# A two-layer decoder trunk on one core: GpSimd gives up its elementwise work, a norm of the second token tile goes to ScalarE, and the block behind a norm runs its matmul passes in another order

## The chip, the cores and the metric

The kernel runs on one core of one Trainium2 chip. The metric is device time in microseconds of one execution, the median of several runs.

The engines are called by these names: PE is TensorE (matmuls and transposes; PEld is its weight load), DVE is VectorE, ACT is ScalarE, POOL is GpSimd, SP is SyncE, whose queue (SPq) issues the transfers. Each engine works through its own queue in order.

## The reference, cut to what matters

256 tokens of 2048 channels pass two layers. Every sub-layer ends in a norm of the residual sum.

```
layer 0:  h = LN(a*h + [pool_mixer | stick_breaking_attention] @ even_w_out)
          h = LN(a*h + (silu(h @ Wg) * (h @ Wu)) @ Wd)                 # 5632 wide
layer 1:  h = LN(a*h + spatial_gating(gelu(h @ odd_w_in)) @ odd_w_out)
          logits = h @ w_router ; the two largest of 8, softmax over them -> gates
          h = LN(a*h + sum_e gates[:, e] * swiglu_e(h))                # 1408 wide
LN(x) = (x - mean) * rsqrt(var + 1e-5) * g + b,    a = 4 ** 0.25,  all in float32
```

## The kernel before, in words

The 256 tokens are two tiles of 128 (t = 0 and 1; `h0_1534` and `h1_1535` in the order's rows). Each product in float32 precision is made of three passes. A chunk of weights, up to 4 k-slices of 128 x 512, comes by a transfer on SP into `raw`. ScalarE rounds it to the head `wh` (L109), VectorE takes the remainder `wl = raw - wh` (L117). The activations are split the same way into `xh` (L161) and `xl` (L162). For each k-slice TensorE runs head times head (L126), head times weight remainder (L127) and activation remainder times weight head (L128). There are 5 `raw` buffers, 4 each of `wh` and `wl`, 4 PSUM tiles for sums (`acc`) and 4 for the rest (`ps`).

A *block* is one tile's 16 k-slices against one chunk column of 512: 48 matmuls, four groups (kg0 to kg3) of four k-slices. Blocks follow each other through all stages, so TensorE only waits where a block's operands come late. That is at the three places where a norm lies between two matmuls:

- **A**, the start of the FFN (about 300 to 340 us): tile 0 is normed while tile 1's last out-projection block still runs. The first FFN block (tile 0) starts while tile 1's norm is done. `ln_to_lhs` normalises a quarter `h` (L239), transposes it on TensorE (L168), scales it on ScalarE and splits it into `xh` and `xl`. Each of the four quarters q0 to q3 holds the four k-slices of one group.
- **B**, the start of the SGU (about 1036 to 1080 us): the same.
- **C**, the start of the experts (about 1328 to 1375 us): the router's logits, top-2, a one-hot matrix `Dt` (L795) of the sorted tokens, and then a gather: matmuls of the tokens' head and remainder (`xth`, `xtl`, made by `token_parts`, L619 and L620) with `Dt` (L813), whose result ScalarE casts to the experts' `xe` (L815). `keep_busy` (L886) issues matmuls on constants there.

A scheduler sets the order within each engine's queue from the program's order and its own due times. `self.plan` is the hand on it: each entry is popped by one `load` and says behind which instruction that chunk's `wl` may stand (a fence without a semaphore, `after`) and on which engine it is made. After a norm of tile 0 the second chunk's `wl` goes to GpSimd as two 128x1024 pieces (A, B and C). In the experts' down projection, the third chunk of each column has three k-slices: VectorE takes two of them, GpSimd the last (`tail=HALF`, 32 chunks). GpSimd also makes five of the eight `xtl`, scales one quarter of tile 1 in C, and does 5 of the 12 multiplications and additions of the final norm behind the last matmul (L744 and L745).

Of the kernel before, what the change touches and what calls it, by code (L numbers as in the profile page):

```python
# [22 lines left out]
CB = 512  # L23
# [8 lines left out]
PIECE = 4  # L32
HALF = 2
FINAL_POOL = ((1, 3), (1, 3))
FINAL_POOL2 = ((1,), ())
RSQRT_MAGIC = float(0x5F3759DF)
# [38 lines left out]
class Trunk:  # L75
# [22 lines left out]

    def load(self, src, w=CB, tail=None):

        nc = self.nc
        fence, planned = self.plan.pop(0) if self.plan else (None, nc.vector)
        src = src.rearrange("p (k n) -> p k n", n=w)
        kc = src.shape[1]
        raw = self.praw.tile([P, kc, w], F32, tag="raw", name="raw")
        wh = self.pw.tile([P, kc, w], F32R, tag="wh", name="wh")
        wl = self.pw.tile([P, kc, w], F32R, tag="wl", name="wl")
        nc.sync.dma_start(raw, src)
        nc.scalar.copy(wh, raw)  # L109
        if tail is not None:  # L110
            cuts = [(0, tail, nc.vector), (tail, kc, nc.gpsimd)]
        elif planned is nc.gpsimd:
            cuts = [(k, min(k + HALF, kc), planned) for k in range(0, kc, HALF)]
        else:
            cuts = [(0, kc, planned)]
        for a, b, eng in cuts:
            self.after(eng.tensor_tensor(wl[:, a:b, :], raw[:, a:b, :], wh[:, a:b, :].bitcast(F32), ALU.subtract),  # L117
                       fence)
        return wh, wl, kc
# [4 lines left out]
    def mm3(self, acc, xh, xl, wh, wl, first, last):  # L124
        mm = self.nc.tensor.matmul
        mm(acc, xh, wh, start=first, stop=False)  # L126
        mm(acc, xh, wl, start=False, stop=False)  # L127
        mm(acc, xl, wh, start=False, stop=last)  # L128

    def blocks(self, groups, lhs, tiles, w=CB, between=None, at=8):  # L130
# [94 lines left out]
    def ln_to_lhs(self, t, stats, which, xT):  # L225

        nc = self.nc
        mean, rstd = self.rstd(stats)
        self.plan += [(self.last, nc.vector)] * (6 if t else 1)
        if t == 0:  # L230
            self.plan += [(None, nc.gpsimd)]
        gc, bc = self.lncols[:, 2 * which, :], self.lncols[:, 2 * which + 1, :]
        for half in range(2):
            xh = self.unit("xh")
            xl = self.unit("xl")
            for q in range(2):
                n = half * 2 + q
                hs = self.h[t][:, n * CB:(n + 1) * CB]
                nc.vector.tensor_scalar(hs, hs, mean, rstd, ALU.subtract, ALU.mult)  # L239
                ps = self.transpose4(hs).rearrange("p (c t) -> p c t", c=4)  # L240
                f = self.pln.tile([P, 4, P], F32, tag="lnT", name="lnT")
                for j in range(4):
                    c = n * 4 + j
                    nc.scalar.activation(f[:, j, :], ps[:, j, :], AF.Identity, bias=bc[:, c:c + 1],
                                         scale=gc[:, c:c + 1])
                self.split_evac(f, xh[:, q * 4:q * 4 + 4, :], xl[:, q * 4:q * 4 + 4, :])
            xT[t, half] = (xh, xl)
# [218 lines left out]
    def ffn(self, xT, G, B, norm):  # L466
# [3 lines left out]
        with self.pool("ffn", side="right") as pf:  # L470
            def gate_up(j):
                accs = {}
                hT = {}
                for u in range(2):
                    groups = self.loads(i["even_ffn_gu"][j, u])
                    for t in range(NT):
                        accs[u, t] = self.block(groups, lhs, t)
                        if j == 1 or (j == 0 and u == 1):
                            self.flush(self.lo_ins)
                        if u == 1:  # L480
                            hT[t] = self.swiglu(pf, accs[0, t], accs[1, t], CB, 4, "f")
                return hT
# [39 lines left out]
    def sgu(self, xT, G0, B0):  # L522
# [3 lines left out]
        with self.pool("sgu", side="right") as pg:  # L526
# [8 lines left out]
            for n in range(8):  # L535
# [8 lines left out]
                for t in range(NT):  # L544
                    acc = self.block(groups, lhs, t)
                    if n < 4:
# [69 lines left out]

    def token_parts(self, src, dst, q, eng):
        cs = slice(q * CB, (q + 1) * CB)
        self.nc.scalar.copy(dst[0][:, cs], src)  # L619
        eng.tensor_tensor(dst[1][:, cs], src, dst[0][:, cs].bitcast(F32), ALU.subtract)  # L620

    def moe(self, pm, stats, G, B):
# [13 lines left out]
        for t in range(NT):  # L636
            mean, rstd = self.rstd(stats[t])
            if t == 0:
                self.plan += [(self.last, nc.vector), (None, nc.gpsimd)]
            nmr = self.nmr(mean, rstd)  # L640
            hs = [self.h[t][:, n * CB:(n + 1) * CB] for n in range(NCB)]
            if t:
                for n in (0, 2, 1, 3):
                    nc.scalar.activation(hs[n], hs[n], AF.Identity, bias=nmr, scale=rstd)
                nc.gpsimd.tensor_tensor(hs[2], hs[2], G[2], ALU.mult)
                nc.gpsimd.tensor_tensor(hs[2], hs[2], B[2], ALU.add)
            lrow = pm.tile([P, NEXP], F32, tag="lrow", name="lrow", bufs=1)
# [5 lines left out]
            if t == 0:  # L653
                for n in range(NCB):
                    self.ln_apply(hs[n], mean, rstd, G[n], B[n])
                    self.token_parts(hs[n], xtok[t, n // 2], n % 2, nc.gpsimd)
        fence = self.last
        self.plan += [(fence, nc.vector)] * 2
        self.keep_busy(8, self.c[:, :CB // 2].bitcast(BF16))
# [13 lines left out]
        for n in range(NCB):  # L673
            if n % 2:
                self.after(nc.vector.tensor_tensor(hs[n], hs[n], G[n], ALU.mult), fence)
                self.after(nc.vector.tensor_tensor(hs[n], hs[n], B[n], ALU.add), fence)
            self.token_parts(hs[n], xtok[1, n // 2], n % 2, nc.gpsimd if n == 2 else nc.vector)
        for t in range(NT):
# [50 lines left out]
    def final_norm(self, stats, G, B):  # L729

        nc = self.nc
        for t in range(NT):
            mean, rstd = self.rstd(stats[t])
            nmr = self.nmr(mean, rstd)
            for n in range(NCB):
                hs = self.h[t][:, n * CB:(n + 1) * CB]
                if n == 0:
                    o2 = self.pw.tile([P, NCB, CB], F32, tag="wh", name="o")
                o = o2[:, n, :]
                if n == 0:  # L740
                    self.ln_apply(hs, mean, rstd, G[n], B[n], o)
                else:
                    nc.scalar.activation(o, hs, AF.Identity, bias=nmr, scale=rstd)
                    (nc.gpsimd if n in FINAL_POOL2[t] else nc.vector).tensor_tensor(o, o, G[n], ALU.mult)  # L744
                    (nc.gpsimd if n in FINAL_POOL[t] else nc.vector).tensor_tensor(o, o, B[n], ALU.add)  # L745
                nc.sync.dma_start(self.out[t * P:(t + 1) * P, n * CB:(n + 1) * CB], o)
# [104 lines left out]
    def expert_down(self, e, gat, p, hT, first, stats, step=None):  # L851
# [5 lines left out]
        for n in range(NCB):  # L857
# [3 lines left out]
            for k in range(0, EXP_KC, PIECE):  # L861
                o, kc = k * CB * P, min(PIECE, EXP_KC - k)
                src = i["odd_moe_down"][e, n][o:o + kc * CB * P].rearrange("(p m) -> p m", p=P)
                groups.append(self.load(src, tail=HALF if kc < PIECE else None))
            acc = self.block(groups, lhs, 0)
# [140 lines left out]
```

## Time and profile before

| | |
|---|---|
| median of 3 runs | 2195.15 us (2191.74 to 2196.63) |
| profiled execution | 2192.12 us, its span 2190.4 us |
| granted TensorE clock, mean of the span | 0.991 |
| busy: PE, DVE, ACT, POOL | 98%, 67%, 52%, 4% |

The profiled execution lies 3.0 us under the median, and 1.7 us of it lie outside the span. Times in the rows are microseconds from the start of the span. The granted clock is given as a share of full speed, 2.4 GHz: 0.50 is the lower level of 1.2 GHz.

### The profile page before, as it was taken

The numbers are of one execution on the slowest core, as the hardware profiler recorded it, in microseconds if no ns is written. First come the engines' busy times: TensorE is split into PE (matmuls) and PEld (weight loads), VectorE is DVE, ScalarE is ACT, GpSimd is POOL, SyncE is SP. The second block draws the span as 40 slices with busy tenths as digits, with TensorE's granted clock in tenths as the row PEclk, the third lists the DMA queues.
The fourth block names the chain that finished last, engine by engine and source line by source line (L and its number), as shares of the span: only waits on it lengthen the run. The fifth ranks groups of instructions, "written<-read, shape, count | busy, mean of one in ns | idle before, by whom it ended". The sixth has DMA issues, their size and how long they took to land.

```text
span 2190.4 us, 24556 instructions
## 1 busy us (share of the span) xinstructions
PE 2147.6 (98%) x9956; PEld 1783.0 (81%) x9956; DVE 1469.1 (67%) x1216; ACT 1143.4 (52%) x954; POOL 96.4 (4%) x56
## 2 busy tenths in 40 slices
PE   9999999999999999999999998999999999999995
PEld 7888878888888888888788886888888888888884
DVE  5444476554454654456776458888889888878988
ACT  5445355343333433343643335766766767676673
POOL 0000010000000000000100002010100100010102
PEclk9999999999999999999999999999999999999998
DMA  9544645555454554455554543899989999998995
GB/s 354 207 154 151 234 154 204 219 192 190 156 218 166 211 192 180 186 191 193 211 192 174 212 164 108 324 351 350 334 333 361 345 337 342 349 344 323 368 356 191
DMA packets 82199, 537.81 MB, mean 246 GB/s; under 512 B 9504, under 2 KB 10656, under 8 KB 28192
## 3 DMA queue, kind: packets, MB, share of 16 engines
q1 hardware_dynamic: 82080, 536.18, 65.8%
q8 instruction: 80, 1.31, 0.2%
q14 instruction: 39, 0.32, 0.0%
HBM read 534.04 MB, written 2.10 MB: 245 GB/s over the span
## 4 chain that ended last, share of the span: by engine, by line
PE 94%; DVE 5%; issue 0%; ACT 0%; DMA 0%; SPq 0%; POOL 0%; DVEq 0%; ACTq 0%; POOLq 0%
PE acc L127 29%; PE acc L128 29%; PE acc L126 29%; PE ps L168 2%; PE ps L813 1%; DVE wl L117 1%; PE ps L872 1%; PE ps L873 1%; DVE xl L162 0%; DVE stats L223 0%; DVE h L221 0%; PE ps L560 0%; PE ps L433 0%; DVE h L212 0%; DVE o L744 0%
## 5 line engine op out<-in xcount | busy, mean ns | idle before, releaser
L117 DVE TENSOR_TENSOR wl<-raw,wh 128x2048 fp32r<-128x2048 f32 (+1 forms) x516 | 1113.5, 2176 | 395.2 <-ACT wh L109 392.8
L109 ACT CAST wh<-raw 128x2048 fp32r<-128x2048 f32 (+2 forms) x519 | 935.7, 1824 | 446.4 <-PE acc L128 408.7
L127 PE MATMUL acc<-wl,xh 128*128 128x512 f32 x960 | 376.6, 392 | 5.4 <-DVE wl L117 5.4
L128 PE MATMUL acc<-wh,xl 128*128 128x512 f32 x960 | 374.8, 390 | 0.9 <-DVE xl L162 0.9
L126 PE MATMUL acc<-wh,xh 128*128 128x512 f32 x960 | 374.6, 390 | 0.5 <-ACT wh L109 0.5
L127 PE MATMUL acc<-wl,xe 128*128 128x512 f32 (+1 forms) x768 | 286.5, 373 | 0.1
L128 PE MATMUL acc<-wh,xe 128*128 128x512 f32 (+1 forms) x768 | 285.5, 372 | 0.0
L126 PE MATMUL acc<-wh,xe 128*128 128x512 f32 (+1 forms) x768 | 284.5, 371 | 0.0
L127 PE MATMUL acc<-wl,hTh 128*128 128x512 f32 x704 | 278.2, 395 | 0.8 <-DVE wl L117 0.8
L128 PE MATMUL acc<-wh,hTl 128*128 128x512 f32 x704 | 277.8, 395 | 0.0
L126 PE MATMUL acc<-wh,hTh 128*128 128x512 f32 x704 | 275.9, 392 | 0.0
L127 PEld LDWEIGHTS acc<-wl,xh 128*128 128x128 f32 x960 | 180.7, 188 | 43.1 <-DVE wl L117 6.1
L128 PEld LDWEIGHTS acc<-wh,xl 128*128 128x128 f32 x960 | 180.8, 188 | 38.2 <-DVE xl L162 1.3
L126 PEld LDWEIGHTS acc<-wh,xh 128*128 128x128 f32 x960 | 180.5, 188 | 38.6 <-ACT wh L109 1.0
L127 PEld LDWEIGHTS acc<-wl,xe 128*128 128x128 f32 x768 | 144.2, 188 | 21.9 <-DVE wl L117 1.8
L126 PEld LDWEIGHTS acc<-wh,xe 128*128 128x128 f32 x768 | 144.2, 188 | 20.5
L128 PEld LDWEIGHTS acc<-wh,xe 128*128 128x128 f32 x768 | 144.2, 188 | 19.7
L117 POOL TENSOR_TENSOR wl<-raw,wh 128x512 fp32r<-128x512 f32 (+1 forms) x38 | 75.9, 2002 | 1875.2 <-ACT wh L109 1803.6
L127 PEld LDWEIGHTS acc<-wl,hTh 128*128 128x128 f32 x704 | 132.3, 188 | 31.5 <-DVE wl L117 2.8
L126 PEld LDWEIGHTS acc<-wh,hTh 128*128 128x128 f32 x704 | 132.4, 188 | 29.2
L128 PEld LDWEIGHTS acc<-wh,hTl 128*128 128x128 f32 x704 | 132.5, 188 | 27.4
L161 ACT CAST hTh<-ps 128x512 fp32r<-128x512 f32 (+1 forms) x46 | 26.2, 569 | 182.9 <-PE ps L168 182.9
(194 smaller groups left out, 1878.7 us busy)
## 6 DMA issues: line engine op xcount, KB each, us to landing
raw<-in_odd_moe_gu_dram SPq DMA_DIRECT2D x128, 1024.0 KB, 6.6
raw<-in_even_ffn_gu_dram SPq DMA_DIRECT2D x88, 1024.0 KB, 4.8
raw<-in_odd_moe_down_dram SPq DMA_DIRECT2D x64, 1024.0 KB, 7.1
raw<-in_odd_moe_gu_dram SPq DMA_DIRECT2D x64, 768.0 KB, 6.0
raw<-in_even_ffn_down_dram SPq DMA_DIRECT2D x44, 1024.0 KB, 4.8
raw<-in_odd_w_in_dram SPq DMA_DIRECT2D x32, 1024.0 KB, 4.8
raw<-in_even_w_in_dram SPq DMA_DIRECT2D x30, 1024.0 KB, 5.4
raw<-in_odd_moe_down_dram SPq DMA_DIRECT2D x32, 768.0 KB, 6.5
```

Of the source, the lines that this page charges most:

```text
L109: nc.scalar.copy(wh, raw)
L117: self.after(eng.tensor_tensor(wl[:, a:b, :], raw[:, a:b, :], wh[:, a:b, :].bitcast(F32), ALU.subtract), fence)
L126: mm(acc, xh, wh, start=first, stop=False)
L127: mm(acc, xh, wl, start=False, stop=False)
L128: mm(acc, xl, wh, start=False, stop=last)
L161: self.nc.scalar.copy(hi, src)
L168: self.nc.tensor.transpose(ps[:, j * P:(j + 1) * P], src[:, j * P:(j + 1) * P], self.ident)
L813: mm(o, xtok[t, c // 8][part][:, cs], Dt[t].rearrange("p a b -> p (a b)"), start=j == 0 and t == 0, stop=t == 1, skip_group_check=True)
L872: nc.tensor.matmul(ps, DT[:, t, :], yh, start=True, stop=False)
L873: nc.tensor.matmul(ps, DT[:, t, :], yl, start=False, stop=True)
```

## The change

All elementwise work leaves GpSimd for VectorE. Plan entries become fences alone. In `ln_to_lhs` tile 1 is normalised by ScalarE (scale `rstd`, bias `nmr = -mean * rstd`). The first block behind a norm in A and B is built by `heads_first`: per group both passes that use the weight head come first, and the passes with `wl` follow one group later. In the MoE start, all of `token_parts` and the affine work on quarters 1 to 3 of tile 1 stand behind the gather's one-hot matrix, the two tiles by turns.

```diff
-    def load(self, src, w=CB, tail=None):
+    def load(self, src, w=CB):
-        fence, planned = self.plan.pop(0) if self.plan else (None, nc.vector)
+        fence = self.plan.pop(0) if self.plan else None
-        if tail is not None:
-            cuts = [(0, tail, nc.vector), (tail, kc, nc.gpsimd)]
-        elif planned is nc.gpsimd:
-            cuts = [(k, min(k + HALF, kc), planned) for k in range(0, kc, HALF)]
-        else:
-            cuts = [(0, kc, planned)]
-        for a, b, eng in cuts:
-            self.after(eng.tensor_tensor(wl[:, a:b, :], raw[:, a:b, :], wh[:, a:b, :].bitcast(F32), ALU.subtract),
-                       fence)
+        self.after(nc.vector.tensor_tensor(wl, raw, wh.bitcast(F32), ALU.subtract), fence)
+    def heads_first(self, groups, lhs, t):
+        acc, mm = self.acc(), self.nc.tensor.matmul
+        n = sum(g[2] for g in groups)
+        k0, late = 0, []
+        def remainders():
+            for k, wl in late:
+                mm(acc, lhs(k, t)[0], wl, start=False, stop=k == n - 1)
+            late.clear()
+        for wh, wl, kc in groups:
+            now = []
+            for j in range(kc):
+                xh, xl = lhs(k0 + j, t)
+                mm(acc, xh, wh[:, j, :], start=k0 + j == 0, stop=False)
+                mm(acc, xl, wh[:, j, :], start=False, stop=False)
+                now.append((k0 + j, wl[:, j, :]))
+            remainders()
+            late += now
+            k0 += kc
+        remainders()
+        return acc
@@ ln_to_lhs
-        self.plan += [(self.last, nc.vector)] * (6 if t else 1)
-        if t == 0:
-            self.plan += [(None, nc.gpsimd)]
+        self.plan += [self.last] * (6 if t else 2)
+        nmr = self.nmr(mean, rstd) if t else None
-                nc.vector.tensor_scalar(hs, hs, mean, rstd, ALU.subtract, ALU.mult)
+                if t:
+                    nc.scalar.activation(hs, hs, AF.Identity, bias=nmr, scale=rstd)
+                else:
+                    nc.vector.tensor_scalar(hs, hs, mean, rstd, ALU.subtract, ALU.mult)
@@ ffn, sgu
-                        accs[u, t] = self.block(groups, lhs, t)
+                        accs[u, t] = (self.heads_first if j == u == t == 0 else self.block)(groups, lhs, t)
-                    acc = self.block(groups, lhs, t)
+                    acc = (self.heads_first if n == t == 0 else self.block)(groups, lhs, t)
@@ moe
-                self.plan += [(self.last, nc.vector), (None, nc.gpsimd)]
+                self.plan += [self.last]
-                nc.gpsimd.tensor_tensor(hs[2], hs[2], G[2], ALU.mult)
-                nc.gpsimd.tensor_tensor(hs[2], hs[2], B[2], ALU.add)
-                    self.token_parts(hs[n], xtok[t, n // 2], n % 2, nc.gpsimd)
+                h0 = hs
-        self.plan += [(fence, nc.vector)] * 2
+        self.plan += [fence] * 3
@@ moe, behind the gather's one-hot matrix
-            if n % 2:
+            if n:
-            self.token_parts(hs[n], xtok[1, n // 2], n % 2, nc.gpsimd if n == 2 else nc.vector)
+            self.token_parts(h0[n], xtok[0, n // 2], n % 2, fence)
+            self.token_parts(hs[n], xtok[1, n // 2], n % 2, fence)
@@ final_norm
-                    (nc.gpsimd if n in FINAL_POOL2[t] else nc.vector).tensor_tensor(o, o, G[n], ALU.mult)
-                    (nc.gpsimd if n in FINAL_POOL[t] else nc.vector).tensor_tensor(o, o, B[n], ALU.add)
+                    nc.vector.tensor_tensor(o, o, G[n], ALU.mult)
+                    nc.vector.tensor_tensor(o, o, B[n], ALU.add)
@@ expert_down
-                groups.append(self.load(src, tail=HALF if kc < PIECE else None))
+                groups.append(self.load(src))
```

On TensorE, in the second half of the first FFN block (place A), before: `xh_2069` and `xl_2070` are tile 0's head and remainder of the channels' second half, `wh_2213`/`wl_2214` are kg2's weights, and the four L168 rows transpose tile 1's normalised quarters.

```order
L126 MATMUL acc_2224<-wh_2213,xh_2069 128x512
L127 MATMUL acc_2224<-wl_2214,xh_2069 128x512
L128 MATMUL acc_2224<-wh_2213,xl_2070 128x512
L126 MATMUL acc_2224<-wh_2213,xh_2069 128x512
L127 MATMUL acc_2224<-wl_2214,xh_2069 128x512
L128 MATMUL acc_2224<-wh_2213,xl_2070 128x512
L168 MATMUL ps_2141<-c_79,h1_1535 128x128 x4
L168 MATMUL ps_2154<-c_79,h1_1535 128x128 x4
L168 MATMUL ps_2169<-c_79,h1_1535 128x128 x4
L168 MATMUL ps_2182<-c_79,h1_1535 128x128 x4
```

The same place now, from the last two k-slices of kg2 to the end of the block (L134 is head times head, L135 activation remainder times head, L128 the passes with `wl`, L181 the transposes; `wl_2209`, `wl_2215` and `wl_2221` are the remainders of kg1, kg2 and kg3):

```order
L134 MATMUL acc_2225<-wh_2214,xh_2069 128x512
L135 MATMUL acc_2225<-wh_2214,xl_2070 128x512
L128 MATMUL acc_2225<-wl_2209,xh_2041 128x512 x4
L134 MATMUL acc_2225<-wh_2220,xh_2069 128x512
L135 MATMUL acc_2225<-wh_2220,xl_2070 128x512
L181 MATMUL ps_2143<-c_79,h1_1535 128x128 x4
L134 MATMUL acc_2225<-wh_2220,xh_2069 128x512
L181 MATMUL ps_2156<-c_79,h1_1535 128x128 x4
L135 MATMUL acc_2225<-wh_2220,xl_2070 128x512
L181 MATMUL ps_2171<-c_79,h1_1535 128x128 x4
L128 MATMUL acc_2225<-wl_2215,xh_2069 128x512 x4
L128 MATMUL acc_2225<-wl_2221,xh_2069 128x512 x4
```

The passes with a weight remainder stand four to eight matmuls behind the heads of their group, the last two groups' at the end of the block; the transposes stand among the heads of the last group, and the fourth in the next block.

On VectorE at the same norm, before (`h0_1534` takes its affine work against `gb`, `h1_1535` the last partial sum of the out projection):

```order
L117 TENSOR_TENSOR wl_2201<-raw_2199,wh_2200 128x2048
L255 TENSOR_TENSOR h0_1534<-h0_1534,gb_1942 128x512
L256 TENSOR_TENSOR h0_1534<-h0_1534,gb_1946 128x512
L162 TENSOR_TENSOR xl_2042<-lnT_2049,xh_2041 128x512
L162 TENSOR_TENSOR xl_2042<-lnT_2062,xh_2041 128x512
L219 SCALAR_TENSOR_TENSOR h1_1535<-h1_1535,acc_2001 128x512
```

and now:

```order
L108 TENSOR_TENSOR wl_2203<-raw_2201,wh_2202 128x2048
L270 TENSOR_TENSOR h0_1534<-h0_1534,gb_1942 128x512
L108 TENSOR_TENSOR wl_2209<-raw_2207,wh_2208 128x2048
L175 TENSOR_TENSOR xl_2042<-lnT_2049,xh_2041 128x512
L271 TENSOR_TENSOR h0_1534<-h0_1534,gb_1946 128x512
L232 SCALAR_TENSOR_TENSOR h1_1535<-h1_1535,acc_2001 128x512
L175 TENSOR_TENSOR xl_2042<-lnT_2062,xh_2041 128x512
```

The second chunk's remainder, two pieces on GpSimd before, is one instruction of 128x2048 ahead of the first `xl`.

On ScalarE in the gather of C, before (`xe` are the gathered tokens, `xth` the heads of the tokens, the number the buffer):

```order
L619 CAST xth_8673<-h1_1535 128x512
L619 CAST xth_8675<-h1_1535 128x512
L815 CAST xe_8853<-ps_8854 128x512
L680 CAST gg_8666<-gates_8794 128x8
L815 CAST xe_8853<-ps_8860 128x512
L619 CAST xth_8673<-h1_1535 128x512
L815 CAST xe_8866<-ps_8867 128x512
```

and now:

```order
L634 CAST xth_8675<-h1_1535 128x512
L634 CAST xth_8673<-h0_1534 128x512 x2
L634 CAST xth_8675<-h1_1535 128x512
L634 CAST xth_8677<-h1_1535 128x512
L829 CAST xe_8855<-ps_8856 128x512
L829 CAST xe_8855<-ps_8862 128x512
L829 CAST xe_8868<-ps_8869 128x512
```

The heads of tile 1's second and third quarter, which need VectorE's affine work, stand ahead of the first `xe`, not between the first few.

## Rows read from the trace of the kernel before

**Rows 1.** The page: the chain that ended last, by engine

```profile
PE 94%; DVE 5%; issue 0%; ACT 0%; DMA 0%; SPq 0%; POOL 0%; DVEq 0%; ACTq 0%; POOLq 0%
```

**Rows 2.** PE's waits: tile, releaser, us in total, times, longest

```profile
PE acc L127 <- DVE wl L117: 6.1, 4, 3.1
PE ps L168 <- DVE h L219: 5.7, 1, 5.7
```

**Rows 3.** Windows: busy PE, PEld, DVE, ACT, POOL; PE clock, DMA share, GB/s

```profile
296.00:330.00 34.00, 30.32 (x141) 24.68 (x140) 27.62 (x46) 21.91 (x42) 5.88 (x2) 0.95 0.39 136
...
1036.00:1070.00 34.00, 30.71 (x144) 25.08 (x143) 28.79 (x49) 21.22 (x40) 6.40 (x3) 0.95 0.39 139
...
1328.00:1375.00 47.00, 38.79 (x206) 30.88 (x206) 41.11 (x96) 28.70 (x43) 15.28 (x9) 0.89 0.26 90
1347.10:1357.30 10.20, 8.37 (x29) 5.37 (x30) 9.55 (x42) 8.11 (x12) 4.68 (x4) 0.50 0.01 4
1359.40:1370.90 11.50, 9.96 (x75) 9.35 (x76) 10.78 (x19) 9.60 (x22) 1.49 (x1) 1.00 0.24 80
1830.00:1870.00 40.00, 40.00 (x181) 33.03 (x180) 38.47 (x27) 28.36 (x20) 6.18 (x4) 1.00 0.98 378
```

**Rows 4.** VectorE at A, in order of time: start, duration, instruction

```profile
304.90 0.68 DVE L255 TENSOR_TENSOR h<-h,gb 128x512 f32<-128x512 f32 x1
...
308.32 2.87 DVE L162 TENSOR_TENSOR xl<-lnT,xh 128x512 fp32r<-128x512 f32 x1
312.29 0.69 DVE L162 TENSOR_TENSOR xl<-lnT,xh 128x512 fp32r<-128x512 f32 x1 [1.09 <-ACT xh L161]
312.90 0.68 DVE L219 SCALAR_TENSOR_TENSOR h<-h,acc 128x512 f32<-128x512 f32 x1
...
317.51 2.29 DVE L117 TENSOR_TENSOR wl<-raw,wh 128x2048 fp32r<-128x2048 f32 x1
```

**Rows 5.** TensorE at A, in order of time

```profile
309.78 0.39 PE L126 MATMUL acc<-wh,xh 128*128 128x512 f32 x1
310.01 0.39 PE L127 MATMUL acc<-wl,xh 128*128 128x512 f32 x1
...
319.85 0.80 PE L127 MATMUL acc<-wl,xh 128*128 128x512 f32 x1 [2.28 <-DVE wl L117]
```

**Rows 6.** TensorE at B, in order of time

```profile
1060.55 0.79 PE L127 MATMUL acc<-wl,xh 128*128 128x512 f32 x1 [3.12 <-DVE wl L117]
```

**Rows 7.** ScalarE at C, in order of time

```profile
1353.50 2.93 ACT L644 ACTIVATE h<-h,nmr,lny 128x512 f32<-128x512 f32 x4 [0.28 <-DVE nmr L205]
```

**Rows 8.** VectorE at C, in order of time

```profile
1338.31 2.34 DVE L649 SCALAR_TENSOR_TENSOR lrow<-rrows,nmr 128x8 f32<-128x8 f32 x1
1340.57 2.96 DVE L212 SCALAR_TENSOR_TENSOR h<-h,lny,gb 128x512 f32<-128x512 f32 x1
...
1348.20 0.68 DVE L219 SCALAR_TENSOR_TENSOR h<-h,acc 128x512 f32<-128x512 f32 x1
...
1353.50 0.23 DVE L649 SCALAR_TENSOR_TENSOR lrow<-rrows,nmr 128x8 f32<-128x8 f32 x1
...
1359.45 0.28 DVE L795 TENSOR_SCALAR Dt<-c,pos 128x128 fp32r<-128x128 f32 x1
```

**Rows 9.** TensorE at C, in order of time

```profile
1370.63 0.39 PE L128 MATMUL acc<-wh,xe 128*128 128x512 f32 x1
```

**Rows 10.** Groups by shape, 1380 to 2130 us: count, busy, mean ns, idle before

```profile
L117 DVE TENSOR_TENSOR wl<-raw,wh 128x1536 fp32r<-128x1536 f32 x64 | 110.0, 1754 | 17.0 <-ACT wh L109 17.0
L117 DVE TENSOR_TENSOR wl<-raw,wh 128x1024 fp32r<-128x1024 f32 x28 | 47.2, 1687 | 1.5 <-ACT wh L109 1.1
```

**Rows 11.** VectorE in the last expert and in the final norm, in order of time

```profile
2134.76 1.23 DVE L117 TENSOR_TENSOR wl<-raw,wh 128x1024 fp32r<-128x1024 f32 x1
...
2175.46 0.74 DVE L212 SCALAR_TENSOR_TENSOR o<-o,lny,gb 128x512 f32<-128x512 f32 x1
```

**Rows 12.** GpSimd in the final norm, in order of time

```profile
2184.17 1.64 POOL L745 TENSOR_TENSOR o<-o,gb 128x512 f32<-128x512 f32 x1 [0.63 <-DVE o L744]
```

More of the change, by code (lines that the diff above doesn't have):

```diff
@@ L33 @@
 HALF = 2
-FINAL_POOL = ((1, 3), (1, 3))
-FINAL_POOL2 = ((1,), ())
 RSQRT_MAGIC = float(0x5F3759DF)
@@ L615, in router_step, with token_parts @@
                              start=k == 0, stop=k == KC - 1)
-    def token_parts(self, src, dst, q, eng):
+    def token_parts(self, src, dst, q, fence):
         cs = slice(q * CB, (q + 1) * CB)
         self.nc.scalar.copy(dst[0][:, cs], src)
-        eng.tensor_tensor(dst[1][:, cs], src, dst[0][:, cs].bitcast(F32), ALU.subtract)
+        self.after(self.nc.vector.tensor_tensor(dst[1][:, cs], src, dst[0][:, cs].bitcast(F32), ALU.subtract), fence)
     def moe(self, pm, stats, G, B):
@@ L642, in moe @@
             if t:
-                for n in (0, 2, 1, 3):
+                for n in range(NCB):
                     nc.scalar.activation(hs[n], hs[n], AF.Identity, bias=nmr, scale=rstd)
-                nc.gpsimd.tensor_tensor(hs[2], hs[2], G[2], ALU.mult)
-                nc.gpsimd.tensor_tensor(hs[2], hs[2], B[2], ALU.add)
             lrow = pm.tile([P, NEXP], F32, tag="lrow", name="lrow", bufs=1)
```

## The prediction

> **What bounds the kernel now.** I read the chain of waits by engine first: 94% of the chain that ended last is TensorE, 5% VectorE [rows 1]. So TensorE's busy stretches can't give anything here (the change keeps the number of its matmuls and alters their order), and the change can win only where TensorE stands still, or lose by making it stand. The list of TensorE's waits says for whom it stands: 6.1 us in four waits for a weight remainder, 5.7 us in one wait for tile 1's residual sum [rows 2]. The windows then say where: at A it is busy 30.32 of 34 us, at B 30.71 of 34, at C 38.79 of 47 [rows 3]. In these windows the granted clock is 0.95, 0.95 and 0.89, so a pause costs a second time: after it TensorE runs at 1.2 GHz for a while. 5% of 34 us is 1.7 us, once at A and once at B; at C 11% of 47 us is 5.2 us, nearly all in the 10.2 us that ran at 0.50. In the steady expert stretch TensorE is busy 40.0 of 40 us, while VectorE is at 38.47 and GpSimd at 6.18 [rows 3]: nothing to win there, but little VectorE time free.
>
> Beside GpSimd's elementwise work VectorE's own instructions are stretched: the remainder `xl` takes 2.87 us while GpSimd makes its two pieces and 0.69 us when it is idle [rows 4]; an instruction on 128x8 elements takes 2.34 us, and 0.23 later [rows 8]; the 128x1024 remainder in the experts' down step averages 1.687 us, and takes 1.23 at a place where GpSimd does nothing [rows 10, 11]. So work taken from GpSimd is partly paid for by VectorE's other work getting faster.
>
> **The change part by part.**
>
> *A, the FFN's start.* It costs 34 - 30.32 = 3.7 us of idle time and 1.7 us of low clock, 5.4 together [rows 3]. After the change VectorE is free of GpSimd and takes the second weight remainder itself (2.29 us, as kg2's [rows 4]; the next instruction starts 2.21 after such a one, and a 128x512 one occupies 0.61, from 312.29 to 312.90). From 304.90: the affine 0.6, kg1's remainder 2.2, the first `xl` 0.6 makes 308.4. It is wanted at 310.0, one pass of 0.23 us behind the block's start at 309.78 [rows 5]; before it came at 311.2. The longer job thus costs nothing and the wait for `xl` goes. Next, tile 1's sum can be added when the out projection ends, at about 310.0, and the statistics and rstd behind it took 4.6 us (312.90 to 317.51 [rows 4]), so rstd is there at 314.6, kg2's remainder at 316.9 and q3's `xl` at 317.5. With heads first, kg2's remainder is not wanted until kg3's heads are through, so the old wait of 2.28 us for it at 319.85 [rows 5] goes. What is late next is q3's `xl`: its first pass stands 33 matmuls behind the start, 309.78 + 33 x 0.23 = 317.3, so 0.3 us. Then tile 1's transposes wait for ScalarE, which now normalises: 0.73 us for each quarter (2.93 for four [rows 7]), the first at 318.3, then 319.0 and 319.8, against TensorE's own arrival; I count 0.6 us. Queued behind those activations on ScalarE are the scaling and `xh` of tile 1; its last quarter's `xl` falls in the next block, which has 11 matmuls in front of it. New stalls 0.9, too short and too spread to lower the clock as I take it. Gain 5.4 - 0.9 = 4.5; between 1.5 (the clock falls anyway and the stalls double) and 5.4.
>
> *B, the SGU's start.* The same edits, 3.3 + 1.7 = 5.0 us at stake [rows 3]. TensorE stopped at 1060.55 - 3.12 = 1057.4, 25 passes behind the block's start, which is therefore 1051.7 [rows 6]. VectorE's rstd stood at 1060.5 - 2.3 = 1058.2; without one stretched `xl` about 1.1 earlier, 1057.1. Then kg2's remainder (2.2) and q3's `xl` (0.6, and a wait for ScalarE of some tenths): 1060.1. Wanted at 1051.7 + 33 x 0.23 = 1059.2. That is 1.0 us late, and VectorE's queue behind it (kg3's remainder, the other tile's `xl`, then the next chunk's first remainder) makes some 1.8 more by my count, an estimate. Gain 5.0 - 2.8 = 2.2; between 0 and 5.
>
> *C, the experts' start.* Tile 1's last sum stands at 1348.20 on VectorE, behind four instructions stretched by GpSimd: two of them took 2.34 and 2.96 us and would take 0.23 and 0.74 [rows 8, 11]: 4.3 us of stretch, and about 1.8 more, an estimate, in the two of L212's form behind them. Now kg0's and kg1's remainders share the queue, and I get the sum at 1343.3, 4.9 earlier. The second chain (statistics, top-2, one-hot) has 3.1 us of stretch by the same reading, and 1.0 us of new waits, as tile 1's transposed copy now stands behind a weight cast on ScalarE. So `Dt`, done at 1359.7 [rows 8], comes at 1352.8. But the work that GpSimd did beside that chain now comes behind `Dt` on VectorE: 8 `xtl` and 6 affine instructions at 0.61 and one weight remainder of 2.3 ahead of the last `xtl`, 8.5 + 2.3 + small ones = 11.0 us, so the last token remainder is there at 1363.8. ScalarE has the heads of tile 1's middle quarters, which need that affine work, ahead of the first `xe` casts; with 4 `ps` buffers TensorE then stands about 3.2 us in the gather. Behind the last `xtl` TensorE has about 2.9 us of gather and casts: the experts start at 1366.7. Before, their first pass in an uninterrupted run was at 1370.63 + 0.23, with five or six already done inside the gather [rows 9]: equal to a start at 1369.5. That is 2.8 us won, less 1.9 (a little over A's 1.7) for a new stretch of low clock behind the pause in the gather, which now runs at 1.00 [rows 3]: gain 0.9. The ends: 6 won (no pause), 4.8 lost (the whole gather at half clock).
>
> *The final norm.* TensorE is done and the end is the last addition. Before: GpSimd's at 2184.17 + 1.64 = 2185.8 [rows 12]. Now 12 instructions on VectorE, 0.61 each, behind its last fused one at 2175.46 + 0.74 = 2176.2 [rows 11]: 2183.5. ScalarE's six activations at 0.73 start before and stay ahead. Gain 2.3 (1.8 to 2.6); the output transfers follow as before.
>
> *The experts' down step.* 32 remainders grow from 128x1024 to 128x1536, which is measured at 1.754 us [rows 10]: 0.07 us longer than the stretched 1.687, 2.2 us of VectorE in all. TensorE's 40.0 of 40 us hides it, VectorE at 38.47 still has 1.5 us in 40. I take 0.
>
> Sum: 4.5 + 2.2 + 0.9 + 2.3 = 9.9 us. Against the profiled execution, 2192.1 - 9.9 = 2182.2; that execution lies 3.0 under the median, so the median of runs should be about 2185.
>
> **The rivals.**
>
> *All clean.* The stalls I count at B and in the gather don't occur, because the scheduler's positions leave more room than my chains: A 5.4, B 5.0, C 6.0, final norm 2.5, 18.9 together: 2176. For it: every stretched instruction returns to its short duration. Against: the order puts the ScalarE heads ahead of the casts.
>
> *The gather falls to the low clock.* The pause of 3.2 us comes ahead of the gather, and the gather's 9.96 busy us [rows 3] then run largely at 1.2 GHz: C loses 4.8 in place of winning 0.9, total 4.2, 2191. For it: at A, B and C a pause of 2.3 us or more was followed by low clock. Against: before, `keep_busy` kept TensorE working up to `Dt`, and the gather ran at 1.00 despite a wait for `xtl`. The Trainium skill, "TensorE: Matmul & The Clock Gate", section "A second HAM failure mode: psum-queue depth-cycling", speaks against the change here: groups of matmuls that cycle through PSUM buffers leave the engine idle for moments, and the clock swings between its levels. The gather is such a cycle; before, this trace does not agree with it (1.00 throughout). By that rule the time is this rival's.
>
> *Idle time changes hands.* ScalarE, now with norm, scaling and heads in one queue, is late for transposes and `xe` by what VectorE gains; only noise is left: 2195. Against: its window shares at A and B are 21.9 and 21.2 of 34 us [rows 3].
>
> *The down step becomes VectorE-bound* (slower). If the measured 1.687 is not stretch but the true duration at that place, or the 1.23 us one already prevailed, a piece that grows by 1.754 - 1.23 = 0.52 us in 32 steps costs 16.6 us with no slack left: 2185 + 16.6, about 2201 or 2202. It decides from the point where VectorE exceeds 40 us per 40 us of TensorE, and 1.5 us are left. For it: 38.47 of 40. Against: GpSimd's 6.18 us in those 40 [rows 3] no longer stretch the neighbours.
>
> **How the numbers follow.** The forecast 0.57, all clean 0.14, the gather at low clock 0.14, idle time changes hands 0.06, the down step bound 0.09. A measurement here tells 0.2%, 4.4 us, from no change, so faster means under 2190.8. Faster: 0.55 of the forecast, 0.14, and half of the low-clock case, 0.07, makes 0.76. Same: 0.02 + 0.07 + 0.06 = 0.15. Slower: 0.09. The range takes in both gainful cases and the low-clock one with their unknowns: 2174 to 2196; the forecast alone 2179 to 2190.
>
> **What would show it.** At A and B the low-clock stretch at the end of the first block should be gone (clock 0.98 or more in those windows) and TensorE's list of waits should have no 2.3 and 3.1 us for a weight remainder; the wait for tile 1's sum at C should shrink from 5.7 us to about 1. In the gather I expect a pause of some 3 us behind the first `xe` casts. The last addition should end some 7 us behind the last fused instruction. VectorE's 128x8 and 128x512 instructions should show no duration over 1 us. The forecast is wrong if TensorE waits for weight remainders in the experts, or if the window at C is no shorter.

## The result, and the profile after

The changed kernel takes 2180.22 us (median of 6 runs, 2179.07 to 2181.67); the kernel before, on the same chip, 2195.67 us (6 runs, 2191.74 to 2196.63). The ratio is 0.9932, 95% interval 0.9919 to 0.9945. The profiled execution took 2179.94 us, span 2178.2, against 2192.12 and 2190.4 before.

Both traces have 9956 matmuls, and at the borders between stages the same ones have been done. So the start of the n-th matmul in one trace less its start in the other tells what a stage gained, to about 0.1 us where no transfer decides. The table has this difference, stage by stage, against the profile of before (minus is shorter); the borders are the matmuls that began there at 300.1, 345.0, 1036.1, 1090.0, 1320.0, 1380.2 us and the last one (2168.57). "Start" is all that lies ahead of the first border. All kernels of the experiments are in it. The traces of the last two have 9955 matmuls: the record of one `keep_busy` matmul at C is missing, and it is counted as if it were there.

| kernel | start | A | FFN | B | SGU | C | experts | behind the last matmul | span |
|---|---|---|---|---|---|---|---|---|---|
| after | +0.1 | -5.3 | 0.0 | -1.7 | +0.1 | -2.9 | -0.6 | -2.0 | 2178.2 |
| no heads first | +0.9 | -4.3 | +0.1 | -0.6 | +0.1 | -2.9 | -0.4 | -2.1 | 2181.2 |
| norm on VectorE | +0.7 | -5.6 | +0.1 | -3.7 | +0.4 | -3.1 | -1.5 | -2.1 | 2175.7 |
| second chunk on GpSimd | +0.2 | -1.7 | 0.0 | -1.7 | +0.1 | +2.0 | -0.4 | -2.0 | 2186.9 |
| before, heads first | +1.1 | -2.1 | 0.0 | +0.3 | 0.0 | +1.9 | +0.3 | 0.0 | 2192.0 |
| GpSimd in down step and end | -0.7 | -5.3 | +0.1 | -1.6 | 0.0 | -2.8 | +1.5 | 0.0 | 2181.7 |
| gather by quarters | +1.8 | -5.3 | +0.1 | -1.6 | 0.0 | -5.0 | -0.8 | -2.0 | 2177.6 |
| token parts early | +0.5 | -5.3 | +0.1 | -1.7 | +0.1 | -2.6 | -1.8 | -2.0 | 2177.6 |
| before again | +0.5 | 0.0 | +0.1 | 0.0 | +0.1 | 0.0 | +0.5 | 0.0 | 2191.5 |
| norm on VectorE and quarters | +1.4 | -5.6 | -0.1 | -3.7 | +0.4 | -5.7 | +0.9 | -2.1 | 2176.0 |
| the same, token parts early | +0.9 | -5.6 | 0.0 | -3.7 | +0.2 | -4.7 | -0.5 | -2.0 | 2175.1 |

The kernel before, profiled twice, agrees within 0.1 us in A, B, C and at the end, and differs by 0.5 in the start and the experts.

TensorE's waits after (to hold against [rows 2]): tile, releaser, us in total, times, longest.

```profile
PE ps L827 <- ACT xe L829: 3.1, 1, 3.1
...
PE ps L827 <- DVE gates L794: 1.8, 1, 1.8
PE acc L117 <- DVE wl L108: 1.7, 2, 1.1
...
PE acc L135 <- DVE xl L175: 1.0, 1, 1.0
PE ps L181 <- DVE h L232: 0.8, 1, 0.8
```

The 6.1 us for weight remainders are 1.7 (1.1 at B, 0.6 in an expert), the 5.7 us for tile 1's sum 0.8; the longest wait is a new one, for ScalarE's casts in the gather. The windows after, with the columns of [rows 3]:

```profile
296.00:330.00 34.00, 34.00 (x166) 27.76 (x165) 25.95 (x45) 27.55 (x49) 0.00 (x0) 1.00 0.46 170
1036.00:1070.00 34.00, 32.75 (x157) 25.93 (x155) 24.53 (x41) 29.93 (x52) 1.09 (x1) 1.00 0.58 217
1070.00:1090.00 20.00, 18.92 (x83) 15.50 (x83) 13.24 (x12) 8.19 (x7) 0.00 (x0) 1.00 0.56 210
1321.30:1368.30 47.00, 40.61 (x219) 33.73 (x219) 39.59 (x105) 30.87 (x45) 0.00 (x0) 0.89 0.26 93
```

At A nothing idles and the clock stays at 1.00. At B it stays at 1.00 too, but 1.3 us of idle time are left and 1.1 us more have appeared in the next window. The clock at C is 0.89 as before.

VectorE and TensorE at A, in order of time, against [rows 4, 5]:

```profile
307.80 0.68 DVE L175 TENSOR_TENSOR xl<-lnT,xh 128x512 fp32r<-128x512 f32 x1
...
314.56 2.29 DVE L108 TENSOR_TENSOR wl<-raw,wh 128x2048 fp32r<-128x2048 f32 x1
316.76 0.68 DVE L175 TENSOR_TENSOR xl<-lnT,xh 128x512 fp32r<-128x512 f32 x1
```

```profile
317.50 0.50 PE L135 MATMUL acc<-wh,xl 128*128 128x512 f32 x1
318.42 0.66 PE L181 MATMUL ps<-c,h 128*128 128x128 f32 x4
```

The first `xl` ends at 308.5, q3's at 317.4, and the first transposes of tile 1 start at 318.4: the chain that the prediction wrote down (308.4, 317.5, 318.3).

### The profile page after: what moved, and what is told of

It reads as the page before. It is cut to its first block, busy times and chain, and to the rows that moved or that the text cites. A ratio compares the mean times of both kernels' runs of the same rounds, so it can differ in the third digit from the quotient of the medians.

```text
span 2178.2 us, 24443 instructions
## 1 busy us (share of the span) xinstructions
PE 2144.2 (98%) x9956; PEld 1780.5 (82%) x9956; DVE 1457.7 (67%) x1225; ACT 1146.9 (53%) x962; POOL 1.6 (0%) x6
## 4 chain that ended last, share of the span: by engine, by line
PE 94%; DVE 3%; ACT 1%; DMA 1%; issue 1%; SPq 0%; DVEq 0%; ACTq 0%
PE acc L117 29%; PE acc L118 29%; PE acc L116 29%; PE ps L181 2%; PE ps L827 1%; DVE wl L108 1%; PE ps L886 1%; PE ps L887 1%; ACT wh L107 1%; ACT lnT L259 0%; DMA raw<-in_odd_moe_down_dram 0%; PE ps L575 0%; PE acc L629 0%; PE ps L448 0%; DMA raw<-in_odd_moe_gu_dram 0%
## 5 line engine op out<-in xcount | busy, mean ns | idle before, releaser
L108 DVE TENSOR_TENSOR wl<-raw,wh 128x2048 fp32r<-128x2048 f32 (+2 forms) x519 | 1121.2, 2178 | 394.9 <-ACT wh L107 393.7
L107 ACT CAST wh<-raw 128x2048 fp32r<-128x2048 f32 (+2 forms) x519 | 935.2, 1824 | 444.9 <-PE acc L118 410.2
L117 PE MATMUL acc<-wl,xh 128*128 128x512 f32 x928 | 363.1, 391 | 1.1 <-DVE wl L108 1.1
L116 PE MATMUL acc<-wh,xh 128*128 128x512 f32 x928 | 361.4, 390 | 0.1
L118 PE MATMUL acc<-wh,xl 128*128 128x512 f32 x928 | 361.3, 390 | 0.0
L117 PEld LDWEIGHTS acc<-wl,xh 128*128 128x128 f32 x928 | 174.2, 188 | 37.1 <-DVE wl L108 1.5
L116 PEld LDWEIGHTS acc<-wh,xh 128*128 128x128 f32 x928 | 174.1, 188 | 37.1 <-ACT xh L174 0.5
L118 PEld LDWEIGHTS acc<-wh,xl 128*128 128x128 f32 x928 | 174.2, 188 | 36.0 <-DVE xl L175 0.2
L118 PEld LDWEIGHTS acc<-wh,xe 128*128 128x128 f32 x768 | 144.2, 188 | 19.8
L116 PE MATMUL acc<-wh,x0h 128*128 128x512 f32 x256 | 103.7, 408 | 1.9 <-ACT wh L107 1.9
```

The source lines that it names most:

```text
L108: self.after(nc.vector.tensor_tensor(wl, raw, wh.bitcast(F32), ALU.subtract), fence)
```

## The experiments

**Pass order undone.**

```diff
-                        accs[u, t] = (self.heads_first if j == u == t == 0 else self.block)(groups, lhs, t)
+                        accs[u, t] = self.block(groups, lhs, t)
```

(and the same in `sgu`).

> The changed kernel with the first block behind a norm in triples again (A and B). Theory 1, VectorE freed from GpSimd carries A and B and the pass order only a part: kg2's remainder, done at 316.85 us at A, is wanted 25 passes behind the block's start, at 315.5, so a pause of about 1.4 us; at B it is done at 1054.4 and wanted at 1052.1, 2.3 us in place of the 1.0 for the activation remainder. A 1.1 to 1.4 and B about 1.3 longer than in the changed kernel, plus 1.7 each if the clock falls behind such a pause: 2 to 6 us in all. Rival, the pass order is the whole gain of A and B: about 7 us longer.

Measured 2183.4 us (0.995, 0.993 to 0.9969); A and B each 1.0 us longer than after. TensorE at A and B:

```profile
317.67 0.50 PE L117 MATMUL acc<-wl,xh 128*128 128x512 f32 x1 [1.18 <-DVE wl L108]
...
1056.44 0.50 PE L117 MATMUL acc<-wl,xh 128*128 128x512 f32 x1 [2.31 <-DVE wl L108]
```

The pauses are 1.2 and 2.3 us where theory 1 had 1.4 and 2.3. The granted clock stayed at 1.00 at A and fell at B (0.95 over 1036 to 1070). The pass order is worth 2 of the 7 us of A and B, the low end of theory 1's range.

**Tile 1's normalisation on VectorE again.**

```diff
-                if t:
-                    nc.scalar.activation(hs, hs, AF.Identity, bias=nmr, scale=rstd)
-                else:
-                    nc.vector.tensor_scalar(hs, hs, mean, rstd, ALU.subtract, ALU.mult)
+                nc.vector.tensor_scalar(hs, hs, mean, rstd, ALU.subtract, ALU.mult)
```

> The changed kernel with tile 1's normalisation on VectorE again. Theory 1: ScalarE's four activations (2.9 us) are what makes the next chunk's first weight head late at B, so the 1.8 us which B gives back in its third block shrink to under 0.5, and A stays within 0.3: about 1 us shorter in all. Rival: the 1.7 us more on VectorE push kg3's remainder behind its pass at A and B, 1 to 1.7 us longer at each: 2 to 3 us longer in all.

Measured 2178.84 us (0.993, 0.991 to 0.9949): A 0.3 and B 2.0 us shorter than after. ScalarE at B in the changed kernel:

```profile
1062.44 0.86 ACT L252 ACTIVATE h<-h,nmr,lny 128x512 f32<-128x512 f32 x1
1063.15 0.66 ACT L174 CAST xh<-lnT 128x512 fp32r<-128x512 f32 x1
1063.82 1.28 ACT L563 ACT_TABLE_LOAD   x1
1065.12 0.60 ACT L563 ACTIVATE sguv<-acc 128x512 f32<-128x512 f32 x1
1065.61 1.50 ACT L259 ACTIVATE lnT<-ps,lncols 128x128 f32<-128x128 f32 x4
1066.98 1.93 ACT L107 CAST wh<-raw 128x2048 fp32r<-128x2048 f32 x1
```

and with the normalisation on VectorE:

```profile
1065.29 0.60 ACT L559 ACTIVATE sguv<-acc 128x512 f32<-128x512 f32 x1
1065.78 0.61 ACT L174 CAST xh<-lnT 128x512 fp32r<-128x512 f32 x1
1066.29 5.53 ACT L107 CAST wh<-raw 128x2048 fp32r<-128x2048 f32 x3
```

In the changed kernel tile 1's last normalisation pushes its scaling behind the GELU and its table load, and the next chunk's head starts at 1067.0, with the rest of tile 1 between it and the one behind it. In the other the heads run through from 1066.3. The late head shows as this wait of TensorE in the changed kernel, the next chunk's first remainder:

```profile
1071.29 0.50 PE L117 MATMUL acc<-wl,xh 128*128 128x512 f32 x1 [1.08 <-DVE wl L108]
```

It is gone in the other kernel. So this part of the change cost 2.3 us; theory 1 holds, with 2.3 us where it expected 1. The medians (2178.84 and 2180.22) are too close to show this by themselves. The table does: B is -3.7 in all three kernels with the normalisation on VectorE, and -1.6 or -1.7 in the four with it on ScalarE and nothing else changed up to B (after, GpSimd in down step and end, gather by quarters, token parts early).

**The second chunk's remainder on GpSimd again** (A, B and C).

```diff
-        self.plan += [self.last] * (6 if t else 2)
+        self.plan += [self.last] * 6 if t else [self.last, "gpsimd"]
...
+        if fence == "gpsimd":
+            for a in range(0, kc, HALF):
+                nc.gpsimd.tensor_tensor(wl[:, a:a + HALF, :], raw[:, a:a + HALF, :],
+                                        wh[:, a:a + HALF, :].bitcast(F32), ALU.subtract)
```

> The changed kernel with the second weight remainder behind each norm on GpSimd again (A, B and C). Theory 1, VectorE's instructions stretch again beside GpSimd: the first activation remainder at A comes at about 311 us instead of 308.5 and is wanted at 310.1, 1 us of pause; at C tile 1's sum comes 2 us or more later: A 1 to 3 longer, B 1 to 2 longer, C 1 to 3 longer, 3 to 8 us in all. Rival: with the heads first the second chunk's remainder is wanted a group later, so GpSimd's slower work is hidden: under 1 us in all.

Measured 2192.13 us (0.9987, 0.9977 to 0.9996): 8.7 us of span longer than after, A 3.6, B 0, C 4.9. The profiled execution is the quickest of ten; by the medians it is 11.9 us. VectorE in this kernel, at A and at C:

```profile
308.54 2.87 DVE L180 TENSOR_TENSOR xl<-lnT,xh 128x512 fp32r<-128x512 f32 x1
```

```profile
1335.30 2.35 DVE L667 SCALAR_TENSOR_TENSOR lrow<-rrows,nmr 128x8 f32<-128x8 f32 x1
...
1337.57 2.96 DVE L230 SCALAR_TENSOR_TENSOR h<-h,lny,gb 128x512 f32<-128x512 f32 x1
```

The stretched durations are back within 0.01 us [rows 4, 8], with only the two GpSimd instructions put back in each place. C waits 3.9 us for tile 1's sum again. So this is the part that carries A and C. At C the granted clock is lower too, 0.85 over 1328 to 1375, so part of the 4.9 us may be the clock's. At B it is worth nothing beside ScalarE's normalisation: this kernel waits 2.1 us for ScalarE's `h` there, the changed one 1.0 and 1.1 us in two other places.

**Only the pass order, on the kernel before** (`heads_first` as in the change, its two calls).

> The kernel before with only the new pass order in the first block behind a norm. Theory 1, both parts are needed: the first activation remainder at A still comes at 311.2 us and is now wanted one pass earlier, but kg2's remainder is wanted some 2.5 us later, so of the waits of 2.3 and 3.1 us at A and B about 2 us each go: 2 to 3.7 us shorter at A, 2 to 3 at B. Rival, the order alone does it: A and B as short as in the changed kernel (5.2 and 1.7 shorter). Other rival: 0, since the wait moves to the activation remainders.

Measured 2192.2 us (0.999, 0.998 to 0.9999). A gains 2.1, most of it by the clock (1.00 over 296 to 330, where before had 0.95; TensorE's busy time there is 30.96 us, before 30.32). B gains nothing (there TensorE waits 1.9 and 0.6 us for tile 1's `h`), and C, whose instructions stand in the same order as before, is 1.9 longer. In its gather:

```profile
1359.00:1368.00 9.00, 7.98 (x41) 7.41 (x42) 9.00 (x16) 5.93 (x12) 1.49 (x1) 0.62 0.07 7
```

The granted clock is 0.62, where it was 1.00 before [rows 3]. Theory 1 holds at A only. The longer C need not be the edit's: the profiled execution (2193.76 us, mean clock 0.990) is one of four at 0.989 or 0.990, which take 2193.76 to 2195.32 us; the other six, at 0.991 or 0.992, take 2191.16 to 2192.79, and no trace shows their C.

**GpSimd back in the down step and in the final norm** (`tail=HALF` for the third chunk, the five final operations).

> The changed kernel with GpSimd's share of the experts' down step and of the final norm as before. Theory 1: the stretch behind the last matmul grows by 2.0 us again, and the experts' 740 us stay within 0.6, because TensorE's work hides either form: 2 us longer in all. Rival: the experts' stretch is 1 us or more shorter or longer with GpSimd in it, so that the changed kernel lost or won something there.

Measured 2185.23 us (0.9949, 0.9932 to 0.9966). The end is 2.0 us longer than after, as expected. The experts are 2.1 us longer than after, 1.5 of them at one wait for a weight remainder in the last expert:

```profile
2122.82 0.50 PE L121 MATMUL acc<-wl,hTh 128*128 128x512 f32 x1 [1.54 <-DVE wl L111]
```

The 8 kernels that share the changed one's expert code lie between -1.8 and +0.9 in this stage, the 4 with GpSimd in it between 0 and +1.5. The means differ by 1.2 us; whether the down step gained is not settled by single profiles.

**The gather by quarters.**

```diff
             self.token_parts(hs[n], xtok[1, n // 2], n % 2, fence)
+            gat[3](n)
...
-        for q in range(4):
-            gat[3](q)
```

> The changed kernel with each quarter of the gather written behind the token parts that it needs, so that ScalarE's first casts of gathered tokens stand ahead of the heads of tile 1's second and third quarter. Theory 1, the 3.1 us pause in the gather is ScalarE's queue order and decides the experts' start: C gets 2 to 4 us shorter. Rival, VectorE's chain of remainders behind the one-hot matrix decides (its last one is done at 1356.5 us), so the pause is hidden by it: C within 1 us.

Measured 2177.92 us (0.9913, 0.9896 to 0.993); C is 2.1 us shorter than after. TensorE's first expert pass, before the gather is through:

```profile
1351.48 0.63 PE L116 MATMUL acc<-wh,xe 128*128 128x512 f32 x1
```

The changed kernel's stands behind the whole gather, at 1359.86. The wait of 3.1 us for a cast is gone. Theory 1 holds, at the low end. The rival does not: VectorE's last remainder is done at 1361.4 here, some 3 us later than in the changed kernel when the stages ahead are taken off, and C is shorter all the same. The 2.1 us are not the pause's price alone: the edit also lets expert passes into the gather, and the granted clock is 0.93 over the 47 us window in which the changed kernel has 0.89. How much each gives is not separated.

**Tile 0's token remainders ahead of the one-hot matrix.**

```diff
+                    self.token_parts(hs[n], xtok[t, n // 2], n % 2, None)
...
-            self.token_parts(h0[n], xtok[0, n // 2], n % 2, fence)
```

> The changed kernel with tile 0's four token remainders on VectorE ahead of the one-hot matrix, as before (there on GpSimd). Theory 1: VectorE idles only 1.1 us ahead of tile 1's sum, so 2.4 us more put the sum about 1.3 us later, and 2.4 us less behind the one-hot matrix bring the last remainder about 1.1 us earlier: C 1 us shorter to 1 longer, so where they stand matters little. Rival: the chain of tile 1 is what counts, C 1.3 to 3 us longer.

Measured 2179.64 us (0.9923, 0.9907 to 0.994); C 0.3 us longer than after. Where they stand matters little, as theory 1 had it.

**The kernel before again.**

> The kernel before, unchanged, for a second profile of it. Theory 1: the first profile was a quick execution (2192.1 against a median of 2195.7), and a slower one spends the difference of some 3 us in the experts' stretch, where the weight transfers are busiest. Rival: it spends it in the pauses at A, B and C, where the changed kernel wins; then the changed kernel's gain there is larger than the two profiles show.

Measured 2196.17 us (0.9998, 0.9988 to 1.0008), its profiled execution 2193.21. Again the profiled one is at the low end (2192.74 to 2197.83), and it shows 0.5 us more each in the start and the experts. Neither theory gets the 3 us from a trace. But the mean granted clock of every execution is on record. Of the ten here, six at 0.989 or 0.990 take 2195.75 to 2197.83 us; four at 0.991, the profiled one among them, take 2192.74 to 2195.26. By an estimate from these rounded shares, 0.002 of 2190 us is 4.4 us, enough for the whole difference. So TensorE's clock goes with it; at which place it falls stays open, as both profiled executions of this kernel are at 0.991.

**Both improvements together**, and with the token parts early.

> The changed kernel with both edits that helped alone: tile 1's normalisation on VectorE (A 0.3 and B 2.0 us shorter than in the changed kernel) and the gather by quarters (C 2.1 shorter). They lie at different places, so theory 1 says they add: A -5.6, B -3.7, C -5.0 against the kernel before, 4.4 us under the changed kernel, a median near 2176. Rival: the places are coupled by the clock or by the weight transfers ahead of them, and one of the two gains falls under half.

> The same, and tile 0's token remainders ahead of the one-hot matrix. Theory 1: with the gather by quarters VectorE's and ScalarE's work behind the one-hot matrix is what paces it, so 2.4 us less of it there is worth more than the 1.3 us that tile 1's sum comes later: C up to 1 us shorter than with quarters alone. Rival, as when it was tried alone: C the same within 0.3, or longer.

Measured 2176.95 us (0.9921, 0.9907 to 0.9934) and 2176.31 us (0.9917, 0.9904 to 0.9931). A, B and C are 0.3, 2.0 and 2.8 us shorter than after in the first, so the two edits add where they are. With the token parts early C gives 1.0 us back and the medians don't differ. At C the granted clock goes the same way: over 47 us (1318 to 1365) it is 0.96 in the first and 0.93 in the second, so differences of 1 us there need not come from the order of the queues. Of the 5.1 us the medians show 3.3; the start and the experts vary by that much from profile to profile. Both beat the kernel before. Their medians lie under the changed kernel's, but the intervals of the three ratios overlap.

## Why the prediction was right

The forecast was 2185, the range 2174 to 2196; measured 2180.2. By the profiled executions the gain is 12.2 us where the sum said 9.9; by the medians it is 15.4, since the profiled execution of before lay 3.5 us under its median. The prediction had corrected for 3.0 of that by adding it to both sides, which is right only if the changed kernel's profile lies as far under its own median. It lies 0.3 under, and its six executions are all at a mean clock of 0.992 to 0.994; where the kernel before was run again, its slower executions are the ones with a lower mean clock. The correction took a property of that kernel's executions for one of both kernels.

*A*: 5.3 for a forecast of 4.5. Each time of the chain came within 0.2 us. Only the term "new stalls 0.9" was too large: in the 34 us window none is seen, the pauses at 317.5 and 318.4 being some tenths. No clock was lost. The undone parts give: GpSimd's share 3.6, the pass order 1.0, and ScalarE's normalisation -0.3. They add up to 4.3, so about 1 us belongs to no single part.

*B*: 1.7 for 2.2. The first new stall was forecast at 1.0 and is this row, so the count of 33 passes held:

```profile
1055.10 0.50 PE L135 MATMUL acc<-wh,xl 128*128 128x512 f32 x1 [1.02 <-DVE xl L175]
```

The second was called 1.8 and put on VectorE's queue; matmul by matmul the trace gives 1.8 back between 1067 and 1072, but its cause is ScalarE's queue: the price of the moved normalisation, which the sum had counted at A only as a wait for transposes. That the size came out is luck.

*C*: 2.9 for 0.9, the step that was mis-sized. VectorE and TensorE in the changed kernel:

```profile
1345.24 0.48 DVE L809 TENSOR_SCALAR Dt<-c,pos 128x128 fp32r<-128x128 f32 x2
...
1355.81 0.69 DVE L635 TENSOR_TENSOR xtl<-h,xth 128x512 fp32r<-128x512 f32 x1
```

```profile
1337.27 0.66 PE L181 MATMUL ps<-c,h 128*128 128x128 f32 x4 [0.78 <-DVE h L232]
...
1351.72 1.22 PE L827 MATMUL ps<-Dt,xtl 128*128 128x256 f32 x4 [3.09 <-ACT xe L829]
...
1358.43 1.12 PE L827 MATMUL ps<-Dt,xtl 128*128 128x256 f32 x8
...
1359.86 0.39 PE L116 MATMUL acc<-wh,xe 128*128 128x512 f32 x1
```

Add the 6.7 us by which this trace is ahead (A and B): `Dt` done at 1352.4 (forecast 1352.8), the last `xtl` at 1363.2 (1363.8), the pause 3.1 (3.2), the experts at 1366.6 (1366.7). The failed term is the 1.9 us for a new stretch of low clock behind the pause. None came. Before, about 10 us at 0.50 lay ahead of the gather (1347 to 1357, the gather from 1359.4) and the gather ran at 1.00 [rows 3]. Now there is again one such stretch of 10 us, and the gather, from 1345.3, lies in it for its first part:

```profile
1344.60:1354.70 10.10, 6.24 (x26) 5.69 (x27) 10.10 (x24) 6.07 (x13) 0.00 (x0) 0.50 0.00 0
1352.70:1355.50 2.80, 2.80 (x18) 2.80 (x17) 2.80 (x5) 2.41 (x5) 0.00 (x0) 0.63 0.00 0
```

It began before the pause (1348.6 to 1351.7) and was over 3 us behind it. What it cost there is little, because ScalarE was late as well: its last head waits for VectorE's affine work, and the casts that free TensorE's `ps` buffers stand behind it:

```profile
1352.98 0.62 ACT L634 CAST xth<-h 128x512 fp32r<-128x512 f32 x1 [0.33 <-DVE h L689]
1353.50 6.76 ACT L829 CAST xe<-ps 128x512 fp32r<-128x512 f32 x13
```

TensorE's passes come in groups of four, one `ps` buffer each. The fourth group, at 1351.72, waited for the first cast, so the seventh needs the fourth cast, the first of these 13, which ends at about 1354.1. The seventh began at 1354.45. By these rows the low clock cost about 0.4 us, an estimate, in place of 1.9. From 1354.8 on TensorE ran at 1.00 without a pause up to the experts. VectorE's last remainder, which the prediction took for the end of the chain, was there at 1356.5, and the passes that use it stand in the row at 1358.43: nothing waited for it. That the experts' start came within 0.1 us of the forecast is therefore partly luck: 2.9 us were put behind that remainder, and 3.4 came.

*The final norm*: 2.0 for 2.3. VectorE's last fused operation and its last two additions:

```profile
2165.23 0.75 DVE L225 SCALAR_TENSOR_TENSOR o<-o,lny,gb 128x512 f32<-128x512 f32 x1
...
2171.91 1.29 DVE L759 TENSOR_TENSOR o<-o,gb 128x512 f32<-128x512 f32 x2
```

12 operations at 0.61 end at 2173.2, and the stretch behind the last matmul is 19.8 us instead of 21.8. *The down step* was taken at 0 and shows 0.6 us less, inside the spread of that stage. TensorE waits once for a weight remainder in the experts, 0.58 us at 1824, where before it waited 0.58 and 0.17. The remainders take what they were forecast to (VectorE's groups from 1370 to 2118 us, count, busy, mean ns):

```profile
L108 DVE TENSOR_TENSOR wl<-raw,wh 128x1536 fp32r<-128x1536 f32 x92 | 159.1, 1754 | 18.8 <-ACT wh L107 18.1
```

One reading behind that forecast was wrong, without harm to it: the 1.23 us for 128x1024 [rows 11] is not a place where GpSimd does nothing. GpSimd's piece starts 0.1 us behind it (the last section has the row), and it is GpSimd that is stretched there.

Of the rivals, the gather's low clock did happen in part (0.50, then 0.63 in the gather), but not behind the pause, and it did not bring that rival's time. The Trainium skill's rule on PSUM cycling ("TensorE: Matmul & The Clock Gate", "A second HAM failure mode: psum-queue depth-cycling") would have the clock swing between its levels in such a gather. This trace does not bear it out: the low level began at 1344.5, in TensorE's wait of 1.8 us ahead of the gather's first pass at 1345.34, and from 1354.8 on the gather went on through the same buffers at 1.00. In the profiled execution of the kernel with only the new pass order the low level fell on the gather later (0.62 over 1359 to 1368), and C is 1.9 us longer there. Work changed hands in one place, B, as the third rival had it. VectorE-bound experts did not come. Of the signs that the prediction named, the clock at A and B, the waits for weight remainders and for tile 1's sum (0.8 us) and the pause in the gather came as stated.

## What to carry to other kernels

Look at the durations of one engine's small instructions while another works: an instruction on 128x8 elements that takes 2.3 us is a sign that the helper engine may cost more than it carries, and moving its work home can be free. Before an operation goes to a less busy engine, list what is queued behind it there; an engine that is half idle over the span can hold the next weight head at just that moment. And before you charge a low clock, look where the stretch begins, and charge it only from the point where TensorE, not another chain, sets the time.

## What the runs showed of the hardware that was not expected

- Of VectorE and GpSimd, the one that started first kept its time and the other was stretched, as two pairs of remainders in the last expert of the kernel before show. At 2134.76 VectorE's 128x1024 starts first and takes 1.23 us [rows 11], GpSimd's 128x512 2.29; at 2141.83 GpSimd's starts first and takes 1.30, VectorE's 2.13:

```profile
2134.86 2.29 POOL L117 TENSOR_TENSOR wl<-raw,wh 128x512 fp32r<-128x512 f32 x1 [70.86 <-ACT wh L109]
2141.83 1.30 POOL L117 TENSOR_TENSOR wl<-raw,wh 128x512 fp32r<-128x512 f32 x1 [4.68 <-ACT wh L109]
```

```profile
2142.08 2.13 DVE L117 TENSOR_TENSOR wl<-raw,wh 128x1024 fp32r<-128x1024 f32 x1
```

- The same instructions in the same order at C ran with a granted clock of 1.00 in the gather of one kernel (before) and 0.62 in that of another (only the pass order), whose stages ahead were 1 to 2 us different. These are single executions, and executions of one kernel differ in their clock as well, so the stages ahead are not shown to be the cause.
- The length of a pause at B does not tell by itself whether the clock falls: pauses of 3.1 us (before), 2.3 us (pass order undone), and 1.9 and 0.6 us (only the pass order) went with 0.95 over 1036 to 1070, one of 2.1 us (second chunk on GpSimd) with 1.00.
- The kernel before varies by 5 us between executions (2192.7 to 2197.8 in ten), and the slower ones have the lower mean clock. The changed kernel varies by 2.6 us in six, but the last kernel of the experiments, which has no elementwise work on GpSimd either, by 4.8 in five (2174.66 to 2179.42). Whether the work on GpSimd has to do with it is open.
